# Scaling the softmax rows one attention slot later: reciprocal and product of P at the head of the next slot

## The chip, the cores and the metric

The kernel runs on one core of one Trainium2 chip. The metric is the device time of one execution in microseconds (us). The core has five engines that work from queues of their own: TensorE multiplies matrices, VectorE and ScalarE work on tiles, GpSimd does a few small things, and SyncE issues most of the transfers. Each engine takes its instructions in the order in which the program gave them out, and waits on semaphores for what others must finish first. "PE", "DVE", "ACT", "POOL" and "SP" in the rows of the profile are TensorE, VectorE, ScalarE, GpSimd and SyncE.

## The reference

One layer of an encoder over 512 tokens of width 2048, in float32:

```python
h = rmsnorm(x, g_mix)
qa, ka, va, qb, kb, vb = split(h @ w_in)
out_a = rmsnorm(mixer_a(qa, ka, va), g_out_a)   # 8 heads, 2 key/value heads, full softmax attention
out_b = rmsnorm(mixer_b(qb, kb, vb), g_out_b)   # 8 heads, three dilated windows merged
x = x + concat(out_a, out_b) @ w_out
gate, up = split(rmsnorm(x, g_ffn) @ w_gate_up)
x = x + (silu(gate) * up) @ w_down
return rmsnorm(x, g_final)
```

In each head `p = softmax(q @ k.T)` over 512 keys, and `o = p @ v`. Mixer B is done by the kernel as the same softmax with an additive mask that holds the logarithm of how often a key is seen by the three windows.

## The kernel before

**Products.** Every float32 matrix is split into a high part (a copy to a reduced format, on ScalarE) and a low part (the difference, on VectorE), and each product is three matrix products into one PSUM bank: high by high, low by high, high by low (`mm3`, lines 238 to 240). The function `split` (lines 229 and 230, or 232 and 233 with a gain) gives out the two instructions one behind the other. For streamed weights the high part is line 290 and the low part line 295; the low part of a weight tile is given out one unit after its high part.

**Units and side work.** The program is one long list of units, each of which multiplies a weight tile with the activations (12 products of 128x512 in the projection and the output projection). The main loop at the end of `encoder_block` goes through the units: it loads ahead, gives out the splits of weights to come (`prepare`), then the products of the unit, and then as much side work as a credit allows. During the projection of mixer B's q and k the credit is 1.42 a unit, from the output projection on 1.9.

**Attention slots.** The attention is side work. There are 16 heads of 4 query tiles, and one slot for each of these 64 tiles, with 9 more at the end; `head_slot(s)` gives out one slot. It does, for different heads and tiles at once: `pt` for slot s - 6 (four transposes of P on TensorE, line 580, then the high and low part of the transposed P, pTh and pTl, lines 229 and 230), `pv` for slot s - 8 (the product with v), `score` for slot s, and ahead of a new head the transposes and splits of q (`tq`) and for mixer B of k (`tk`). `score` multiplies q and k, lets VectorE find the row maxima (line 565 for mixer A, line 569 with the mask for mixer B), ScalarE the exponentials and their row sums (line 566 or 571), and VectorE the reciprocal of the sums (line 573) and P times it, in place (line 574).

Between two slots VectorE's queue gets what the program gives out there: after `tq` and `tk`, extra tasks of the slot (rotary pieces, lines 517 to 521; splits of v), then from `prepare` splits of attention outputs that were read back (class `Back`, lines 232 and 233) and of weights (line 295), and from the units the additions of finished output rows (line 960).

**Banks.** PSUM has 8 banks, kept in one queue: `bank()` takes the first, `release()` appends. A unit's accumulation holds four, the output of the current head one, and the others pass through scores and transposes. `pt` gives its bank back when pTl has been computed, `score` when the maxima (mixer A: the exponentials) have been. In the output projection four banks come free when line 960 has added the rows.

Of the kernel before, what the change touches and what calls it, by code (L numbers as in the profile page):

```python
# [67 lines left out]
def encoder_block(ctx, tc, x, g_mix, w_in, g_q_a, g_k_a, g_out_a, g_out_b, w_out, g_ffn,  # L68
# [15 lines left out]
    def slot(base, dtype=F32, shape=(P, 512)):  # L84
        return sp.tile(list(shape), dtype, tag="s", name=nm(base))
# [11 lines left out]
    def bank():  # L97
        return banks.popleft()

    def release(*tiles):  # L100
        banks.extend(tiles)
# [3 lines left out]
    def small(n=4):  # L105
        used[0] += n
        assert used[0] <= 512
        return smalls[:, used[0] - n:used[0]]
# [127 lines left out]
    def mm3(dst, a, b, start, stop, chained=False):  # L236
        (ah, al), (bh, bl) = a, b
        nc.tensor.matmul(dst, ah, bh, start=start, stop=False, skip_group_check=chained)  # L238
        nc.tensor.matmul(dst, ah, bl, start=False, stop=False, skip_group_check=chained)  # L239
        nc.tensor.matmul(dst, al, bh, start=False, stop=stop, skip_group_check=chained)  # L240

    def cols(pair, lo, n=P):
        return pair[0][:, lo:lo + n], pair[1][:, lo:lo + n]
# [285 lines left out]
    class Head:  # L529
# [27 lines left out]
        def score(self, t):  # L557
            if t == 0:
                self.negm, self.z, self.rz = small(), small(), small()
            ps = bank()  # L560
            mm3(ps, cols(self.q, t * P), self.k, True, True)
            p = slot("p")
            nmx, z, rz = self.negm[:, t:t + 1], self.z[:, t:t + 1], self.rz[:, t:t + 1]
            if self.kind == "A":
                nc.vector.tensor_reduce(nmx, ps, axis=AX.X, op=OP.max, negate=True)
                nc.scalar.activation(p, ps, AF.Exp, bias=nmx, accum_out=z)
            else:
                lo = (NT - 1 - t) * P
                nc.vector.tensor_tensor_reduce(p, ps, mask[:, lo:lo + S], -1.0, 3e38, op0=OP.add, op1=OP.min,
                                               accum_out=nmx)  # L570
                nc.scalar.activation(p, p, AF.Exp, bias=nmx, scale=-1.0, accum_out=z)
            release(ps)
            nc.vector.reciprocal(rz, z)
            nc.vector.tensor_scalar(p, p, rz, None, op0=OP.mult)
            self.p[t] = p

        def pt(self, kb):
            ps = bank()
# [42 lines left out]
    def head_at(slot):  # L621
        h, i = divmod(slot, NT)
        return (heads[h], i) if 0 <= h < len(heads) else (None, i)

    def head_slot(s):
        head, i = head_at(s - TURN_LAG)
        if head:
            head.pt(i)
        head, i = head_at(s - VALUE_LAG)
        if head:  # L630
            head.pv(i)
            if i == NT - 1:
                head.fin()
        head, i = head_at(s)
        if head:
            head.score(i)
        for lead in ("tq", "tk"):
            head, i = head_at(s + {"tq": 4, "tk": 2}[lead])
            if head and i == 0:
                getattr(head, lead)()  # L640
# [8 lines left out]
    def attention_tasks():  # L649
# [38 lines left out]
        for s in range(2 * NHA * NT + VALUE_LAG + 1):  # L688
            cost = 1.5 if s < NHA * NT else 1.2 if s < 2 * NHA * NT else 0.7
            todo += [weighed(cost, lambda s=s: head_slot(s))] + extra.get(s, [])  # L690
# [697 lines left out]
```

## Time and profile before

| | us |
|---|---|
| median of 3 runs | 2010.85 |
| range of the runs | 2010.63 to 2011.96 |
| the profiled execution's own time | 2011.22 |
| span of its instructions | 2009.4 |
| mean granted TensorE clock | 0.997 of full |

The span runs from the first instruction to the last; the rest of the execution's time, 1.8 us, lies around it. A row in order of time gives the start, the duration, the engine, the line of the kernel, the operation, the output and inputs by the program's names, and in brackets how long the engine had stood idle before it and what ended that. Where two instructions of an engine follow closely, the end of one overlaps the start of the next, so the distance from start to start says what one costs. A window row gives the busy time of each engine in a stretch of the span.

### The profile page before, as it was taken

What the parts mean: (1) busy time and instruction counts of PE and PEld (TensorE: products, weight loads), DVE (VectorE), ACT (ScalarE), POOL (GpSimd) and SP (SyncE); (2) the same over time, 40 slices, a digit from 0 to 9 for tenths busy, and PEclk for the clock granted to TensorE, in tenths of its full rate; (3) what the DMA queues carried; (4) which work ended last, traced back from release to release, by engine and by line L of the source; (5) the groups of instructions that cost most, each with busy time, mean ns of one, the idle gap of its engine ahead of it and who ended that gap; (6) DMA issues with size and microseconds to landing.
All of it is one profiled execution on the core that took longest, in us unless ns stands there. A gap on an engine that the chain in (4) does not pass through costs nothing. (4 is left out here: it accounts for less than half of the span.)

```text
span 2009.4 us, 27417 instructions
## 1 busy us (share of the span) xinstructions
PE 1984.8 (99%) x9019; PEld 1632.0 (81%) x9019; DVE 1562.4 (78%) x2781; ACT 1114.6 (55%) x1988; POOL 127.4 (6%) x157
## 2 busy tenths in 40 slices
PE   9999999999999999999999999999999999999998
PEld 7788888887788888888888888888888888788886
DVE  6877876667764698878878878878779987877967
ACT  8655345456544565555555545455555666666656
POOL 0000100000010000000000000000000121111121
PEclk9999999999999999999999999999999999999999
DMA  8577433335344645737647657558467799768765
GB/s 274 179 276 249 159 116 99 106 129 169 96 140 132 209 153 188 279 119 258 241 135 273 208 178 275 168 189 287 141 221 262 195 248 272 187 169 266 200 152 175
DMA packets 231391, 390.61 MB, mean 194 GB/s; under 512 B 21408, under 2 KB 70352, under 8 KB 231120
## 3 DMA queue, kind: packets, MB, share of 16 engines
q1 hardware_dynamic: 204880, 326.13, 48.4%
q0 software_dynamic: 14960, 33.04, 8.1%
q10 hardware_dynamic: 11408, 29.70, 4.2%
q8 instruction: 70, 1.15, 0.2%
q14 instruction: 73, 0.60, 0.1%
HBM read 325.08 MB, written 63.70 MB: 193 GB/s over the span
## 5 line engine op out<-in xcount | busy, mean ns | idle before, releaser
L238 PE MATMUL b<-tw,arena 128*128 128x512 f32 x2136 | 838.4, 392 | 2.2 <-ACT ev L1152 2.2
L239 PE MATMUL b<-tw,arena 128*128 128x512 f32 x2136 | 833.6, 390 | 2.8 <-DVE tw L777 2.6
L240 PE MATMUL b<-tw,arena 128*128 128x512 f32 x2136 | 832.9, 390 | 0.0
L774 ACT ACTIVATE tw<-raw 128x512 fp32r<-128x512 f32 x924 | 558.6, 628 | 436.6 <-DVE raw L814 285.9
L777 DVE TENSOR_TENSOR tw<-raw,tw 128x512 fp32r<-128x512 f32 x924 | 617.8, 685 | 172.4 <-ACT tw L774 169.5
L239 PEld LDWEIGHTS b<-tw,arena 128*128 128x128 f32 x2136 | 401.7, 188 | 89.2 <-DVE tw L777 7.4
L238 PEld LDWEIGHTS b<-tw,arena 128*128 128x128 f32 x2136 | 401.5, 188 | 84.6 <-ACT ev L1152 2.9
L240 PEld LDWEIGHTS b<-tw,arena 128*128 128x128 f32 x2136 | 401.4, 188 | 84.5 <-DVE arena L330 0.5
L814 DVE TENSOR_TENSOR raw<-raw,raw 128x512 f32<-128x512 f32 x528 | 360.5, 683 | 2.0 <-DMA raw<-in_w_gate_up_dram 2.0
L238 PE MATMUL b<-w,arena 128*128 128x512 f32 x368 | 146.1, 397 | 0.0
L239 PE MATMUL b<-w,arena 128*128 128x512 f32 x368 | 143.6, 390 | 0.7 <-DVE w L295 0.7
L240 PE MATMUL b<-w,arena 128*128 128x512 f32 x368 | 143.8, 391 | 0.0
L1153 POOL DMA_DIRECT2D x1d<-ev x76 | 66.4, 975 | 1150.0 <-ACT ev L1152 1135.6
L239 PEld LDWEIGHTS b<-w,arena 128*128 128x128 f32 x368 | 69.2, 188 | 15.3 <-DVE w L295 1.6
L240 PEld LDWEIGHTS b<-w,arena 128*128 128x128 f32 x368 | 69.1, 188 | 14.9
L238 PEld LDWEIGHTS b<-w,arena 128*128 128x128 f32 x368 | 69.2, 188 | 13.5
L774 ACT ACTIVATE tw<-stage 128x512 fp32r<-128x512 f32 x93 | 55.6, 627 | 41.0 <-DVE stage L814 30.6
L777 DVE TENSOR_TENSOR tw<-stage,tw 128x512 fp32r<-128x512 f32 x93 | 61.5, 684 | 13.6 <-ACT tw L774 13.6
L295 DVE TENSOR_TENSOR w<-raw,w 128x512 fp32r<-128x512 f32 x96 | 64.7, 684 | 6.0 <-ACT w L290 3.5
L230 DVE TENSOR_TENSOR pTl<-b,pTh 128x512 fp32r<-128x512 f32 x64 | 43.8, 686 | 29.6 <-ACT pTh L229 26.9
L290 ACT ACTIVATE w<-raw 128x512 fp32r<-128x512 f32 x96 | 58.3, 623 | 15.5 <-PE b L239 6.9
L357 DVE TENSOR_TENSOR pair<-pair 128x256 f32<-128x256 f32 x120 | 45.5, 420 | 26.2 <-ACT pair L1009 25.1
(189 smaller groups left out, 1748.9 us busy)
## 6 DMA issues: line engine op xcount, KB each, us to landing
raw<-in_w_gate_up_dram SPq DMA_DIRECT2D x616, 256.0 KB, 5.3
raw<-in_w_down_dram SPq DMA_DIRECT2D x176, 256.0 KB, 7.1
stage<-in_w_in_dram SPq DMA_DIRECT2D x114, 256.0 KB, 4.8
forms<-pair SPq DMA_DIRECT2D x22, 896.0 KB, 5.3
x1d<-ev POOLq DMA_DIRECT2D x76, 256.0 KB, 6.7
fr<-forms ACTq DMA_DIRECT2D x35, 512.0 KB, 6.1
raw<-in_w_in_dram SPq DMA_DIRECT2D x64, 256.0 KB, 4.4
raw<-in_w_out_dram SPq DMA_DIRECT2D x32, 512.0 KB, 4.7
```

Source lines behind the costliest of these rows:

```text
L230: nc.vector.tensor_tensor(lo, src, f32(hi), op=OP.subtract)
L238: nc.tensor.matmul(dst, ah, bh, start=start, stop=False, skip_group_check=chained)
L239: nc.tensor.matmul(dst, ah, bl, start=False, stop=False, skip_group_check=chained)
L240: nc.tensor.matmul(dst, al, bh, start=False, stop=stop, skip_group_check=chained)
L290: nc.scalar.activation(self.w[0], src, AF.Copy)
L295: nc.vector.tensor_tensor(self.w[1], self.src, f32(self.w[0]), op=OP.subtract)
L357: nc.vector.tensor_tensor(out, x, y, op=op)
L774: nc.scalar.activation(self.pair[:, 0], self.src, AF.Copy)
L777: nc.vector.tensor_tensor(self.pair[:, 1], self.src, f32(self.pair[:, 0]), op=OP.subtract)
L814: nc.vector.tensor_tensor(t[dst], t[src[0]], t[src[1]], op=OP.add if form == "m6" else OP.subtract)
L1153: nc.gpsimd.dma_start(x1_dram[2 * cb + j, row], e, accum_op=OP.add)
```

## The change

The reciprocal and the scaling leave `score` and become a function of their own, which `head_slot` calls for slot s - 1 before anything else of slot s. `score` now ends with the exponentials.

```diff
@@ -570,9 +570,12 @@
                                                accum_out=nmx)
                 nc.scalar.activation(p, p, AF.Exp, bias=nmx, scale=-1.0, accum_out=z)
             release(ps)
+            self.p[t] = p
+
+        def norm(self, t):
+            p, z, rz = self.p[t], self.z[:, t:t + 1], self.rz[:, t:t + 1]
             nc.vector.reciprocal(rz, z)
             nc.vector.tensor_scalar(p, p, rz, None, op0=OP.mult)
-            self.p[t] = p
 
         def pt(self, kb):
             ps = bank()
@@ -623,6 +626,9 @@
         return (heads[h], i) if 0 <= h < len(heads) else (None, i)
 
     def head_slot(s):
+        head, i = head_at(s - 1)
+        if head:
+            head.norm(i)
         head, i = head_at(s - TURN_LAG)
         if head:
             head.pt(i)
```

The order of the instructions on TensorE, ScalarE, GpSimd and in the transfers stays as it was; on VectorE the pair moves behind everything that is given out between two slots, to just ahead of the next slot's pTl.

## The prediction

> **What bounds the kernel now.** I read the page first, then stage windows over the attention, then the groups of VectorE, then the order of time around each stop of TensorE.
>
> From the page, the span and the TensorE total:
>
> ```profile
> span 2009.4 us, 27417 instructions
> ...
> PE 1984.8 (99%) x9019; PEld 1632.0 (81%) x9019; DVE 1562.4 (78%) x2781; ACT 1114.6 (55%) x1988; POOL 127.4 (6%) x157
> ```
>
> Windows (start:end, length, then busy us and instructions of PE, PEld, DVE, ACT, POOL, then clock, DMA share, GB/s):
>
> ```profile
> 254.00:457.00 203.00, 202.99 (x987) 167.36 (x985) 135.29 (x315) 102.54 (x219) 13.50 (x11) 1.00 0.35 114
> 457.00:479.00 22.00, 20.82 (x105) 16.48 (x103) 16.78 (x45) 14.71 (x32) 1.06 (x1) 1.00 0.59 182
> 479.00:507.00 28.00, 24.39 (x115) 19.36 (x113) 21.00 (x50) 15.22 (x31) 1.29 (x1) 0.94 0.42 139
> 507.00:540.00 33.00, 28.95 (x144) 22.71 (x145) 23.90 (x59) 16.29 (x34) 2.59 (x2) 1.00 0.37 112
> 540.00:580.00 40.00, 40.00 (x203) 32.98 (x202) 29.32 (x62) 23.80 (x48) 3.90 (x3) 1.00 0.32 102
> ```
>
> TensorE is the bound nearly everywhere. These five windows hold the attention, and in them TensorE stands still only between 457 and 540: 1.18 + 3.61 + 4.05 = 8.84 us. That is all that a better VectorE order could win, 0.44% of the time. The rest of the attention has no TensorE wait to remove, only margins to lose.
>
> The two moved instructions, grouped (busy, mean ns, idle of the engine just before them and who ended it):
>
> ```profile
> L574 DVE TENSOR_SCALAR p<-p,smalls 128x512 f32<-128x512 f32 x64 | 33.6, 525 | 2.5
> ...
> L573 DVE RECIPROCAL smalls<-smalls 128x1 f32<-128x1 f32 x64 | 10.5, 164 | 59.5 <-ACT p L566 30.1 <-ACT p L571 29.4
> ```
>
> VectorE idles 59.5 us in front of the reciprocals, 0.93 a slot, until ScalarE has finished the exponential. The question is how much of that lies under the 8.84 us. The TensorE stops, in order of time:
>
> ```profile
> 481.56 0.65 PE L580 MATMUL b<-fixed,p 128*128 128x128 f32 x4 [2.42 <-DVE pTl L230]
> 495.96 0.50 PE L238 MATMUL b<-pTh,vh 128*128 128x512 f32 x1 [0.74 <-DVE pTl L230]
> 507.08 0.50 PE L238 MATMUL b<-kTh,qTh 128*128 128x512 f32 x1 [0.52 <-DVE pTl L230]
> 511.71 0.66 PE L580 MATMUL b<-fixed,p 128*128 128x128 f32 x4 [0.45 <-DVE pTl L230]
> ...
> 521.25 0.51 PE L238 MATMUL b<-arena,arena 128*128 128x512 f32 x1 [1.10 <-DVE x L960]
> 525.46 0.65 PE L580 MATMUL b<-fixed,p 128*128 128x128 f32 x4 [0.72 <-DVE qTl L230]
> 527.26 0.51 PE L238 MATMUL b<-kTh,qTh 128*128 128x512 f32 x1 [0.45 <-DVE pTl L230]
> 539.49 0.66 PE L580 MATMUL b<-fixed,p 128*128 128x128 f32 x4 [1.25 <-DVE pTl L230]
> ```
>
> Every one ends with a VectorE instruction, mostly the low part of the transposed P, which gives a PSUM bank back. So what counts is whether that split comes earlier.
>
> **The change part by part.** No instruction is added or removed: 64 reciprocals and 64 scalings change place on VectorE's queue. No queue of DMAs is passed. The order was maximum, reciprocal, scaling, X, pTl of the next slot; it becomes maximum, X, reciprocal, scaling, pTl. X is what the program gives out between two slots: splits of q, k or v, splits of attention rows read back (L233), a weight split (L295), rotary pieces, row additions (L960). What X has to wait for decides. A slot whose X is a q and a v split, first on VectorE, then on ScalarE:
>
> ```profile
> 482.02 0.08 DVE L569 DVE_READ_ACCUMULATOR2_ANT smalls<- 128x1 f32 x1
> 482.99 0.16 DVE L573 RECIPROCAL smalls<-smalls 128x1 f32<-128x1 f32 x1 [0.88 <-ACT p L571]
> ...
> 483.59 0.68 DVE L230 TENSOR_TENSOR qTl<-b,qTh 128x512 fp32r<-128x512 f32 x1
> 484.19 0.68 DVE L230 TENSOR_TENSOR vl<-vraw,vh 128x512 fp32r<-128x512 f32 x1
> 484.79 0.68 DVE L230 TENSOR_TENSOR pTl<-b,pTh 128x512 fp32r<-128x512 f32 x1
> ```
> ```profile
> 482.14 0.72 ACT L571 ACTIVATE p<-p,smalls 128x512 f32<-128x512 f32 x1 [2.15 <-DVE smalls L569]
> ...
> 482.86 0.58 ACT L229 ACTIVATE qTh<-b 128x512 fp32r<-128x512 f32 x1
> 483.34 0.62 ACT L229 ACTIVATE vh<-vraw 128x512 fp32r<-128x512 f32 x1
> ```
>
> Reciprocal and scaling take 0.60 start to start (482.99 to 483.59). ScalarE does the high part of q behind the exponential, until 482.86 + 0.58 = 483.44. Now VectorE does its 0.60 of scaling while that runs. Afterwards it stands at the q split until about 483.48, 1.38 after the end of the accumulator read, wins 0.11 there, and then pays the 0.60 in front of pTl: pTl comes 0.49 later. With L233 first, whose high part (L232) also follows the exponential, nothing is won and pTl comes 0.60 later. If X needs nothing of ScalarE (rotary pieces, L295, whose high part is a step older), VectorE fills the 0.88 and pTl comes up to 0.88 earlier. Empty X: nothing changes.
>
> Now the stops, by the order of X in each slot. The first:
>
> ```profile
> 477.58 0.71 ACT L571 ACTIVATE p<-p,smalls 128x512 f32<-128x512 f32 x1
> ...
> 478.81 0.71 ACT L232 ACTIVATE arena<-oback,fixed 128x512 fp32r<-128x512 f32 x1
> ```
> ```profile
> 479.55 0.75 DVE L233 SCALAR_TENSOR_TENSOR arena<-oback,fixed,arena 128x512 fp32r<-128x512 f32 x1 [0.45 <-ACT arena L232]
> 480.21 0.68 DVE L295 TENSOR_TENSOR arena<-raw,arena 128x512 fp32r<-128x512 f32 x1
> 480.82 0.68 DVE L230 TENSOR_TENSOR pTl<-b,pTh 128x512 fp32r<-128x512 f32 x1
> ```
>
> 1. L233 is held by L232 (478.81 + 0.71), so 479.55 stands; L295 follows, then 0.60, then pTl. The stop of 2.42 becomes 3.02: **+0.60**.
> 2. To 495.96 VectorE runs without waiting for TensorE. The q/v slot shown gives +0.49 (1.09 by then), the next has L233 and L295, +0.60 (1.69), the third a k split, L233, L295, +0.60, but there 0.80 is swallowed by an old wait and its return:
>
> ```profile
> 495.22 0.69 DVE L230 TENSOR_TENSOR pTl<-b,pTh 128x512 fp32r<-128x512 f32 x1 [0.71 <-ACT pTh L229]
> ...
> 502.02 0.75 DVE L233 SCALAR_TENSOR_TENSOR arena<-oback,fixed,arena 128x512 fp32r<-128x512 f32 x1 [0.33 <-ACT arena L232]
> ```
>
> pTl was free to go at 495.22 - 0.71 - 0.09 of gap; 494.42 + 1.69 + 0.60 = 496.71, 1.49 later. TensorE, late by 0.60 already, loses **+0.89**.
> 3. For 507.08 the slot holds a q split, then L233 (held at 502.02 as above): **+0.60**, 2.09 in all.
> 4. The next slot's X is rotary pieces alone:
>
> ```profile
> 507.55 0.08 DVE L569 DVE_READ_ACCUMULATOR2_ANT smalls<- 128x1 f32 x1
> 508.51 0.17 DVE L573 RECIPROCAL smalls<-smalls 128x1 f32<-128x1 f32 x1 [0.88 <-ACT p L571]
> ...
> 510.96 0.69 DVE L230 TENSOR_TENSOR pTl<-b,pTh 128x512 fp32r<-128x512 f32 x1
> ```
>
> 510.96 - 508.51 - 0.60 = 1.85 of work fills the 0.88; pTl is late by 2.09 - 0.88 = 1.21 only, TensorE by 2.09, so the stop of 0.45 goes: **-0.45**, 1.64.
> 5. The row additions at a chunk's end free accumulators:
>
> ```profile
> 519.75 0.40 PE L240 MATMUL b<-arena,arena 128*128 128x512 f32 x1
> ...
> 520.45 1.41 DVE L960 SCALAR_TENSOR_TENSOR x<-b,smalls,x 128x512 f32<-128x512 f32 x2
> ```
>
> The last product ends at 520.15, L960 starts 0.30 later. It can start 0.27 sooner, no more, as it needs that product: **-0.27** of the 1.10, 1.37 in all. The scaling then stands behind the pair, so pTl and the next maximum are late by 1.37 + 0.60 = 1.97.
> 6. The q split after it:
>
> ```profile
> 522.98 0.08 DVE L569 DVE_READ_ACCUMULATOR2_ANT smalls<- 128x1 f32 x1
> ...
> 524.71 0.69 DVE L230 TENSOR_TENSOR qTl<-b,qTh 128x512 fp32r<-128x512 f32 x1
> ```
>
> 523.06 + 1.97 + 1.38 = 526.41 against 524.71, 1.70 later: **+0.33** beyond 1.37.
> 7. Two splits, then 0.60, then pTl: 1.70 + 0.60 = 2.30 late, so 527.26 moves by **+0.60**. The stop before 539.49 follows its own ScalarE chain and moves along unchanged.
>
> Sum +2.3 us on the profiled execution (span 2009.4, time 2011.22): 2013.5. The median of the runs lies 0.37 below that execution, so I forecast 2013.1. A measurement of this kernel tells about 0.2%, 4.0 us, from no change; this is inside.
>
> Costed at nothing: 254 to 457, where VectorE is busy 135.29 of 203 us and TensorE stops 0.01; and 540 to 580. Without that cover each of some five slots with splits or L960 there costs 0.49 to 0.60, at most 2.4 us; a gain is excluded, since TensorE is busy 40.00 of 40.00.
>
> **The rivals.** *The wait goes and none follows.* Were the high parts ready when VectorE reaches X, the stops it ends at 481, 496, 507, 511, 525 and 527 (5.30) and 0.27 at L960 go: 2005.3. It decides from about three quarters of that. Against it: both ScalarE rows of the q/v slot start behind the exponential. Chance 0.10.
>
> *Nothing moves.* VectorE's delays and gains cancel ahead of TensorE: 2010.9. For it: the slots with L295 or rotary pieces alone win what the others lose. Chance 0.16.
>
> *Slower beyond 4 us.* Between 540 and 580 the late pTl meets a TensorE without spare banks: 2.3 + 2.4 = 4.7, 2015.5; it decides from 1.7 of the 2.4. For it: VectorE waits there for little but the exponential. Against: no stop now. Chance 0.16.
>
> *The clock.* After the 2.42 us stop TensorE ran slowly:
>
> ```profile
> 482.00:486.00 4.00, 4.00 (x13) 3.14 (x12) 3.08 (x9) 2.30 (x5) 0.00 (x0) 0.57 0.01 5
> ```
>
> 0.43 x 4.00 = 1.72 us of work lost, now hidden as VectorE sets the pace there. A second such stretch, after a stop that grows to 1.6 near 496 or follows 527, would be uncovered: 2.3 + 1.7 = 4.0, 2014.9, on the bound. Chance 0.08. [...]
>
> **How the numbers follow.** Forecast 0.50. Same: 0.50 + 0.16 + half of the clock's 0.08 = 0.70; slower 0.16 + 0.04 = 0.20; faster 0.10. The range takes in no change, the two slow cases and a little beyond each, and leaves the full gain out: 2009.0 to 2016.0.
>
> **What would show it.** The idle in front of the reciprocals falls from 59.5 us to under 15; instead VectorE waits in front of qTl, kTl, vl and L233 for ScalarE, over 20 us together (24 q and k splits at up to 1.38). The stop near 481 grows to about 3.0, that near 511 goes, the one at L960 shrinks to about 0.8. TensorE's idle from 457 to 540 is about 11. I am wrong if that idle falls below 6, if stops appear before 457 or after 540, or if the q and k splits come without a wait.

## The result and the profile after

| | before | after |
|---|---|---|
| median of 6 runs of each, us | 2012.2 | 2017.33 |
| lowest and highest, us | 2010.63, 2016.39 | 2016.9, 2021.22 |
| the profiled execution: time, span, us | 2011.22, 2009.4 | 2017.18, 2015.4 |
| mean granted TensorE clock | 0.997 | 0.996 |

The ratio is 1.0028, 95% interval 1.0019 to 1.0038: slower by 5 us, where 2.3 were forecast, and above the range's end of 2016.0. Three runs of the kernel before were added here, and its median with them is 2012.2 in place of the 2010.85 above.

The top of the page of the kernel after:

```profile
span 2015.4 us, 27422 instructions
...
PE 1987.7 (99%) x9019; PEld 1634.3 (81%) x9019; DVE 1562.6 (78%) x2781; ACT 1114.2 (55%) x1988; POOL 127.9 (6%) x157
```

The windows of the kernel after, with the columns of the prediction's:

```profile
254.00:457.00 203.00, 203.00 (x989) 167.68 (x988) 136.23 (x314) 101.78 (x216) 13.70 (x11) 1.00 0.35 114
457.00:479.00 22.00, 20.63 (x103) 16.46 (x101) 16.44 (x46) 13.99 (x29) 1.06 (x1) 1.00 0.48 148
479.00:507.00 28.00, 22.55 (x98) 18.13 (x98) 17.43 (x40) 16.53 (x34) 1.29 (x1) 0.88 0.48 166
507.00:540.00 33.00, 30.58 (x144) 23.98 (x144) 25.62 (x64) 14.59 (x31) 1.29 (x1) 0.95 0.33 102
540.00:580.00 40.00, 38.91 (x197) 31.69 (x196) 27.92 (x61) 22.43 (x48) 3.87 (x3) 1.00 0.26 84
```

TensorE stands still for 1.37 + 5.45 + 2.42 = 9.24 us from 457 to 540 (8.84 before), and now for 1.09 from 540 to 580, where it was busy for 40.00 of 40.00. Stops of 9.24 + 1.09 - 8.84 = 1.49 do not make 5 us; the clock of 0.88 and 0.95 (0.94 and 1.00 before) and places outside these windows have a part in it.

VectorE's group of reciprocals, and then its waits from 245 to 585 us (in total, times, the longest), of the kernel after:

```profile
L577 DVE RECIPROCAL smalls<-smalls 128x1 f32<-128x1 f32 x64 | 10.2, 159 | 12.4 <-ACT p L566 6.8 <-ACT p L571 5.7
```
```profile
DVE pTl L230 <- ACT pTh L229: 36.1, 28, 3.0
DVE qTl L230 <- ACT qTh L229: 17.8, 13, 1.4
DVE kTl L230 <- ACT kTh L229: 9.9, 7, 1.5
...
DVE arena L233 <- ACT arena L232: 6.6, 7, 2.7
```

The idle in front of the reciprocals fell from 59.5 to 12.4 us, and VectorE now waits 17.8 + 9.9 + 6.6 = 34.3 us for the high parts of the splits that come first (1.9 before, all of it in front of L233).

**Where the 5 us are.** Each execution is cut at three instructions of TensorE that every kernel has: the first transposes of q (L542), the first transposes of finished output rows (`b<-fixed,x`), and a stop in the down projection that ends with ScalarE's `ev`. The stretch between the first two is the attention and holds every instruction that was moved. In an execution of the kernel before:

```profile
242.83 0.60 PE L542 MATMUL b<-fixed,qA 128*128 128x128 f32 x4
...
644.27 0.60 PE L1006 MATMUL b<-fixed,x 128*128 128x128 f32 x4
```

All parts in us, from rows like these; the labels are those of the experiments, `before` and `after` the executions above:

| kernel | start | attention | behind it | tail | span |
|---|---|---|---|---|---|
| before | 242.56 | 401.37 | 1084.34 | 281.13 | 2009.4 |
| before_second | 242.83 | 401.44 | 1084.68 | 279.75 | 2008.7 |
| before_third | 242.60 | 401.47 | 1084.69 | 278.64 | 2007.4 |
| after | 244.05 | 405.61 | 1085.45 | 280.29 | 2015.4 |
| after_second | 242.66 | 405.18 | 1085.90 | 279.56 | 2013.3 |
| after_third | 242.96 | 405.96 | 1086.27 | 279.81 | 2015.0 |
| e_odd | 242.73 | 401.04 | 1082.51 | 279.82 | 2006.1 |
| odd_third | 243.21 | 401.24 | 1082.21 | 279.64 | 2006.3 |
| e_even | 242.91 | 405.55 | 1084.70 | 280.24 | 2013.4 |
| e_mixerA | 244.43 | 400.31 | 1084.58 | 281.38 | 2010.7 |
| e_last_heads | 243.62 | 403.35 | 1084.69 | 279.54 | 2011.2 |
| last_second | 242.85 | 402.01 | 1085.28 | 279.46 | 2009.6 |
| e_not_last | 242.65 | 403.39 | 1086.08 | 281.58 | 2013.7 |
| not_last_third | 242.88 | 403.48 | 1085.24 | 280.20 | 2011.8 |
| e_behind_score | 243.40 | 397.93 | 1084.21 | 279.46 | 2005.0 |
| e_splits_first | 242.90 | 402.30 | 1085.22 | 279.48 | 2009.9 |
| one_third_head | 242.90 | 402.41 | 1082.12 | 278.77 | 2006.2 |
| one_fifth_head | 244.66 | 401.34 | 1086.15 | 279.95 | 2012.1 |

By the means of the three executions of each, the change costs 405.58 - 401.43 = 4.15 us in the attention and 1085.87 - 1084.57 = 1.30 behind it. Start and tail vary by up to 2.5 us between executions of one kernel; the 1.49 by which the start of the profiled execution after lies later than before's is of that kind, as two other executions of it start at 242.66 and 242.96.

### The profile page after: what moved, and what is told of

Same layout as the page of the kernel before. It is cut to its first block, busy times and chain, and to the rows that moved or that the text cites. A ratio compares the mean times of both kernels' runs of the same rounds, so it can differ in the third digit from the quotient of the medians.

```text
span 2015.4 us, 27422 instructions
## 1 busy us (share of the span) xinstructions
PE 1987.7 (99%) x9019; PEld 1634.3 (81%) x9019; DVE 1562.6 (78%) x2781; ACT 1114.2 (55%) x1988; POOL 127.9 (6%) x157
## 4 chain that ended last, share of the span: by engine, by line
PE 88%; DVE 5%; DMA 3%; ACT 2%; issue 1%; ACTq 0%; POOL 0%; SPq 0%; POOLq 0%; DVEq 0%
PE b L238 28%; PE b L239 28%; PE b L240 28%; DMA raw<-in_w_down_dram 2%; DVE tw L783 2%; PE b L583 1%; DVE raw L820 1%; PE b L1087 1%; DVE arena L1138 0%; ACT tw L780 0%; PE b L319 0%; PE b L1012 0%; DVE pTl L230 0%; DMA x<-x1d 0%; PE b L542 0%
## 5 line engine op out<-in xcount | busy, mean ns | idle before, releaser
L239 PEld LDWEIGHTS b<-tw,arena 128*128 128x128 f32 x2136 | 401.4, 188 | 90.3 <-DVE tw L783 9.1
L238 PEld LDWEIGHTS b<-tw,arena 128*128 128x128 f32 x2136 | 401.4, 188 | 85.3 <-ACT ev L1158 2.9
```

## The experiments

**The new order in the odd tiles alone, and in the even tiles alone.** In the even tiles what the program gives out between two slots begins with a q split (tile 0) or, in mixer B, a k split (tile 2); in the odd tiles with none.

```diff
+            if t % 2 != 1:      # e_even: != 0
+                self.norm(t)
...
         head, i = head_at(s - 1)
-        if head:
+        if head and i % 2 == 1: # e_even: == 0
             head.norm(i)
```

> The deferral for query tiles 1 and 3 of each head only; tiles 0 and 2 scale at once, as before. The splits of q and k are given out in slots of tiles 0 and 2, so here no deferred pair stands behind one. Theory of the waits (the loss comes from the pair queued behind splits that ScalarE has not begun): near the kernel before, -1 to +1.5 us, VectorE's waits in front of qTl and kTl almost gone, the stop near 481 us still about 3.0 as its slot holds a read-back split (L233). Rival of the clock (the loss is the number of half-rate stretches of 1.7 us each, whatever the order): +2 to +5 us, if three stretches stay. Rival that the deferral as such costs: half of the whole change, about +2.5 us.

> The deferral for query tiles 0 and 2 only, the slots with the splits of q and k. Theory of the waits: most of the loss of the whole change, +2 to +5 us, over 20 us of VectorE waits in front of qTl and kTl, and none of the gain in the slots of weight splits alone. Rival that the deferral as such costs: half, about +2.5 us, with no difference to the odd tiles. Rival of the clock: follows the number of half-rate stretches, 1.7 us for each beyond the one of the kernel before.

Measured: the odd tiles alone 2008.18 us, ratio 0.9983 [0.9974, 0.9992]; the even tiles alone 2016.09, ratio 1.0024 [1.0015, 1.0033]. The attention of the even tiles is 4.1 us longer, as in the changed kernel; that of the odd ones 0.2 to 0.4 shorter. So the loss in the attention comes with the slots that begin with a q or a k split. Most of it follows the mechanism of the prediction: VectorE's waits for qTh and kTh (17.8 and 8.4 us with the even tiles) are not there with the odd ones. But 0.86 of the 4.1 arise at one stop, before 542.82, that another cause lengthens (see the part on why the prediction was wrong). The 3 us that the odd tiles win are not in the attention at all: 2.1 to 2.4 of them lie behind it, where nothing was moved. That is taken up below.

**Mixer A alone.**

```diff
+            if self.kind != "A":
+                self.norm(t)
...
-        if head:
+        if head and head.kind == "A":
             head.norm(i)
```

> The deferral in mixer A's heads alone (slots up to about 412 us); mixer B scales at once. Cover as the prediction had it: TensorE has no stop before 457 us although VectorE waits some 10 us in front of qTl there; the time is that of the kernel before, within 1 us. Rival, that the deferral costs in every slot: half of the loss, +2.5 us.

Measured: 2012.27 us, ratio 1.0001 [0.9992, 1.0010]; no stop of TensorE before 457. That part of "costed at nothing" holds. The attention is even 1.1 us shorter than before's, but hardly through the new order: in this execution the clock granted to TensorE is 1.00 from 479 to 507, where before's is 0.94, with one stretch at half rate (0.57 from 482 to 486). What such a stretch is worth is read from `last_second` below.

**The last two heads of mixer B alone, and all but these.** Their slots are the ones behind 534 us.

```diff
+            if self.kind == "A" or self.h < 6:      # e_not_last: kind "B" and h >= 6
+                self.norm(t)
...
-        if head:
+        if head and head.kind == "B" and head.h >= 6:      # e_not_last: not that
             head.norm(i)
```

> The deferral in the last two heads of mixer B alone, about 540 to 570 us. As the prediction costed it: nothing, no stop of TensorE after 540 us. Rival (the cover there is thin, as the changed kernel's two stops at 556 and 558 us say): two stops of 0.8 us together between 550 and 560 us, +0.8 us.

> The deferral everywhere but in the last two heads of mixer B, the complement of the run of those alone. Theory that the stretch after 540 us carries about half of the loss (two stops there, behind a margin of 0.15 us that the kernel before had between the pTl of 550.45 us and the product of 551.29): +1.5 to +3 us over the kernel before, no stop of TensorE after 545 us. Theory that the loss is the sum of the steps up to 527 us: the whole +5. If the half-rate stretches decide: +1.7 for each that later stops don't hide.

The stops of TensorE from 530 to 560 us, first with the last two heads alone, then with all but these:

```profile
540.96 0.66 PE L585 MATMUL b<-fixed,p 128*128 128x128 f32 x4 [1.67 <-DVE pTl L230]
553.72 0.50 PE L238 MATMUL b<-pTh,vh 128*128 128x512 f32 x1 [0.70 <-DVE pTl L230]
555.15 0.50 PE L238 MATMUL b<-kTh,qTh 128*128 128x512 f32 x1 [0.45 <-ACT sq L611]
```
```profile
541.58 0.66 PE L585 MATMUL b<-fixed,p 128*128 128x128 f32 x4 [1.18 <-DVE pTl L230]
```

The stops behind 540 belong to the last two heads, and to nothing else. The attention is 1.98 longer with them alone (403.35 against 401.37) and 1.96 without them (403.39 and 403.48 against 401.47 and less): the two sum to the 4 of the changed kernel. The times say more than that: 2015.92, ratio 1.0017 [1.0008, 1.0026], and 2015.55, ratio 1.0022 [1.0012, 1.0032], 4.9 us each by the medians and 3.4 and 4.4 by the ratios. The rest had to lie outside the attention.

**Both kernels once more on one chip.** No edit.

> The kernel before once more, for a second execution's clock. [...] If the half rate costs its 1.7 us each time, the attention is 1.7 shorter without it.

> The changed kernel once more. The stops near 478, 484 and 499 and those of 556 and 558 us come again within 0.3 us, as VectorE's order makes them; the number of half-rate stretches may differ from three. If the stretches only take the place of later stops, the attention (first transposes of q to first transposes of the output rows, 405.6 us in the first execution) is within 1 us of that; if they add up, 1.7 us shorter for each one less.

> The deferral in the last two heads once more, as the runs' median lies 2.9 us above the execution that was profiled (2013.02). [...]

This pair shows the change cleanest: the starts are 0.17 us apart, and from 455 to 560 both have TensorE at half rate in one stretch only (products of 0.63 us in place of 0.39, starting from 483.13 to 484.83 before and from 483.61 to 485.74 after). The execution of the changed kernel, its two marks of the attention and the stops between them, less two that the kernel before has too (0.64 near 459 and 0.45 near 478):

```profile
242.66 0.60 PE L542 MATMUL b<-fixed,qA 128*128 128x128 f32 x4
...
476.66 0.50 PE L238 MATMUL b<-pTh,vh 128*128 128x512 f32 x1 [0.54 <-DVE pTl L230]
...
482.53 0.85 PE L583 MATMUL b<-fixed,p 128*128 128x128 f32 x4 [3.05 <-DVE pTl L230]
497.80 0.50 PE L238 MATMUL b<-pTh,vh 128*128 128x512 f32 x1 [1.65 <-DVE pTl L230]
509.29 0.50 PE L238 MATMUL b<-kTh,qTh 128*128 128x512 f32 x1 [0.93 <-DVE pTl L230]
522.26 0.50 PE L238 MATMUL b<-arena,arena 128*128 128x512 f32 x1 [0.58 <-DVE x L966]
524.11 0.66 PE L583 MATMUL b<-fixed,p 128*128 128x128 f32 x4 [0.18 <-DVE pTl L230]
526.77 0.66 PE L583 MATMUL b<-fixed,p 128*128 128x128 f32 x4 [0.62 <-DVE qTl L230]
529.16 0.50 PE L238 MATMUL b<-kTh,qTh 128*128 128x512 f32 x1 [1.04 <-DVE pTl L230]
542.26 0.65 PE L583 MATMUL b<-fixed,p 128*128 128x128 f32 x4 [2.10 <-DVE pTl L230]
554.64 0.50 PE L238 MATMUL b<-pTh,vh 128*128 128x512 f32 x1 [0.34 <-DVE pTl L230]
556.06 0.50 PE L238 MATMUL b<-kTh,qTh 128*128 128x512 f32 x1 [0.45 <-ACT sq L609]
...
647.84 0.60 PE L1012 MATMUL b<-fixed,x 128*128 128x128 f32 x4
```

Set against the starts of the same instructions in the kernel before, the shift between the two grows by these steps (the numbers are the prediction's):

| place | start before | start after | shift grows by | predicted |
|---|---|---|---|---|
| a product near 384 | 384.00 | 383.53 | -0.30 | 0 |
| a new stop near 477 | 476.60 | 476.66 | +0.53 | 0 |
| 1 | 481.84 | 482.53 | +0.63 | +0.60 |
| 2 | 496.26 | 497.80 | +0.85 | +0.89 |
| 3 | 507.39 | 509.29 | +0.36 | +0.60 |
| 4 | 512.02 | 513.30 | -0.62 | -0.45 |
| 5 | 521.56 | 522.26 | -0.58 | -0.27 |
| 6 | 525.76 | 526.77 | +0.31 | +0.33 |
| 7 | 527.56 | 529.16 | +0.59 | +0.60 |
| "moves along unchanged" | 539.83 | 542.26 | +0.83 | 0 |
| "costed at nothing" | 552.47 | 556.06 | +1.16 | 0 |
| first output rows | 644.27 | 647.84 | -0.02 | 0 |
| sum | | | +3.74 | +2.3 |

With the last two heads alone, in the execution `last_second`, TensorE's clock is 1.00 in every window from 478 to 490. Two windows of it, below the same two of the kernel before in `before_second` (the clock is the third number from the end):

```profile
482.00:484.00 2.00, 2.00 (x8) 1.71 (x8) 1.08 (x5) 1.57 (x4) 0.00 (x0) 0.50 0.04 13
484.00:486.00 2.00, 2.00 (x7) 1.59 (x6) 2.00 (x4) 0.73 (x2) 0.00 (x0) 0.66 0.00 0
```
```profile
482.00:484.00 2.00, 2.00 (x12) 1.70 (x11) 1.08 (x5) 1.72 (x4) 0.00 (x0) 1.00 0.03 12
484.00:486.00 2.00, 2.00 (x10) 1.64 (x10) 2.00 (x4) 0.59 (x2) 0.00 (x0) 1.00 0.00 0
```

Up to there the order of the two is the same. At 485.26 TensorE is 1.68 us ahead; at the stop near 496, which grew from 0.74 to 1.52, 0.96 of that is left, and 1.21 near 507. So VectorE's chain hides 0.5 to 0.7 of the 1.7 us that the stretch of `before_second` loses (0.50 x 2.00 + 0.34 x 2.00 = 1.68), and 1.0 to 1.2 go through.

**The order with the q and k splits ahead of the score, and the reciprocal behind it.**

```diff
-        head, i = head_at(s)        # e_splits_first: tq and tk stand ahead of score
-        if head:
-            head.score(i)
         for lead in ("tq", "tk"):
             ...
+        head, i = head_at(s)
+        if head:
+            head.score(i)
```
```diff
     def head_slot(s):               # e_behind_score: norm stands behind score, ahead of tq and tk
-        head, i = head_at(s - 1)
-        if head:
-            head.norm(i)
...
             head.score(i)
+        head, i = head_at(s - 1)
+        if head:
+            head.norm(i)
```

> The changed kernel, with one thing taken from what makes VectorE wait: the transposes and splits of q and k of the next head are given out ahead of the slot's score, so that ScalarE's high parts stand ahead of the exponential in its queue. Theory of the waits: VectorE's idle in front of qTl and kTl falls from 27.7 us to under 8, and the loss goes: 3 to 6 us below the changed kernel, at or a little below the kernel before; the stop near 481 us stays about 3, as L233 is not moved. Rival of the clock: as the number of half-rate stretches, whatever these waits do. Rival that the deferral as such costs: as slow as the changed kernel.

> Reciprocal and scaling of the slot before are given out right behind the score of this slot, so the pair runs while the exponential of this slot does and stands in front of the splits again. Theory of the waits: pTl is never later than in the kernel before, and up to 0.88 us earlier in slots without a split; VectorE's idle in front of the reciprocals under 2 us; TensorE's idle in the attention falls from 8.8 to 4 to 6 us, the time by 2 to 6 us below the kernel before. Rival that the deferral as such costs: as slow as the changed kernel, +5 us. Rival of the clock: gains only as the stop near 481 falls so far that its half-rate stretch goes, another 1 us.

Measured: splits ahead of the score 2012.76 us, ratio 1.0006 [0.9997, 1.0016], attention 402.30; no stop is left behind 540, and the waits of L233 double to 12.9 us. Those in front of qTl and kTl fell to 7.3 + 2.3 = 9.6 us, not under 8, and the mean granted clock of this execution is 0.996, against before's 0.997, so the two orders are not compared cleanly by it. Reciprocal and scaling behind the next slot's maxima 2008.24, ratio 0.9984 [0.9975, 0.9992], attention 397.93, which is 3.5 us shorter than before's. It beats both kernels. There the pair fills the time in which ScalarE computes the high parts, and the low parts follow without having been put behind. The stops of TensorE near 511 and 521 are gone, and those near 525 and 539 shrank to 0.49 and 0.42.

**The clock by itself.** Two programs that leave out the whole block and write a copy of an input tile to every output row: dense products on TensorE, broken by stops of VectorE of six lengths and then by pairs of stops (first), or by short stops and runs of transposes (second).

```diff
+        for k in STOPS:                          # e_stops: 0 to 5 additional VectorE additions
+            stop(ps, k)
+            n += 1
+            ps = dense(DENSE + 5 * (n % 4))
...
+        for k, t in ((0, 0), (0, 4), (0, 8), (0, 12), (0, 20), (None, 12), (None, 24), (1, 4)):   # e_turns
+            if k is not None:
+                stop(ps, k)
+                dense(1)
+            turns(t)
+            n += 1
+            ps = dense(DENSE + 5 * (n % 4))
```

> The disputed cost by itself: nothing of the block is computed and the output holds a copy of a tile of x. Runs of 46 to 61 dense 128x512 products are parted by stops in which VectorE does 2 to 7 instructions of 0.6 us (about 1.5 to 4.5 us), six times each; then pairs of stops with 4 or 9 products between them. [...]

> The clock by itself, second part: nothing of the block is computed and the output holds a copy of a tile of x. Dense runs are parted by a stop of 1.1 us followed by 0, 4, 8, 12 or 20 transposes of 128x128, by 12 or 24 transposes without a stop, and by a stop of 1.8 us with 4 transposes, eight times each. [...]

Three stops of the first program, and two windows behind the last of them:

```profile
18.09 11.86 PE L93 MATMUL b<-b,a 128*128 128x512 f32 x51 [1.18 <-DVE a L100]
31.79 13.01 PE L93 MATMUL b<-b,a 128*128 128x512 f32 x56 [1.84 <-DVE a L100]
47.36 13.00 PE L93 MATMUL b<-b,a 128*128 128x512 f32 x49 [2.56 <-DVE a L100]
```
```profile
49.00:50.00 1.00, 1.00 (x4) 0.81 (x3) 0.00 (x0) 0.00 (x0) 0.00 (x0) 0.50 0.00 0
53.00:54.00 1.00, 1.00 (x6) 0.84 (x5) 0.00 (x0) 0.00 (x0) 0.00 (x0) 1.00 0.00 0
```

Behind the stops of 1.18 and 1.84 us the products took 0.23 us each (11.86 for 51, 13.01 for 56). Behind that of 2.56 the 49 took 13.00, 1.6 us longer than at this pace, and the clock in the windows of 1 us from 48 on is 0.90, 0.50, 0.50, 0.50, 0.89 and 1.00: by these, some 0.20 + 3.00 + 0.22 = 3.4 us at half rate. In the second program, 12 and 24 transposes alone (1.47 and 2.79 us of them) were each followed by products of 0.23 us:

```profile
90.97 1.47 PE L106 MATMUL t<-ident,raw 128*128 128x128 f32 x12
92.20 12.98 PE L95 MATMUL b<-b,a 128*128 128x512 f32 x56
105.01 2.79 PE L106 MATMUL t<-ident,raw 128*128 128x128 f32 x24
107.55 14.08 PE L95 MATMUL b<-b,a 128*128 128x512 f32 x61
```

The mean granted clock is 0.906 over the 1093.4 us of the first program and 0.995 over the 959.7 us of the second, so an estimate from the means, with the clock at 1.00 or 0.50 throughout, is that (1 - 0.906) x 2 x 1093.4 = 206 us of the first lie at half rate, and (1 - 0.995) x 2 x 959.7 = 10 us of the second.

In the kernel's own executions the length of a stop does not tell by itself whether half rate follows. With a stop of 2.42 us the clock is 0.57 from 482 to 486 in `before`, and 1.00 from 479 to 507 in `e_mixerA`; with one of 3.06 it is 0.50 from 484 to 486 in `after`, and with one of 3.05 it is 1.00 from 478 to 496 in `not_last_third`. The second program was to explain the stretch of the changed kernel with a stop of 1.04 us (0.50 from 532 to 534 in `after`) and did not; that stays open.

**Does the rest stick to the kernel?** No edit; the same four kernels on one chip.

> The kernel before, looked at once more on the chip of three others, to part the time in three: up to the first transposes of q (about 242.8 us), from there to the first transposes of the output rows (the attention), and from there to the end. Attention theory (all that the change costs lies between 457 and 560 us): the attention is 401.4 us again and the rest 1364 to 1366 us. Rival (something behind the attention, in which no instruction was moved, sticks to a kernel): the rest is 1364.4 again within 0.3, and the changed kernels of this row stay longer.

> The changed kernel once more. Attention theory: the attention is 405.2 us with one stretch at half rate, up to 405.6 with three; stops near 478 [0.54], 498 [1.65], 542 [2.1] and 555 and 556 [0.34 and 0.45] again; the rest lies as the kernel before's of the same row does, 1364 to 1366. Rival: the rest is longer than the other's by 1 us or more.

> The new order everywhere but in the last two heads of mixer B, a second look at this kernel. Attention theory: the attention is 403.4 again, none of its stops after 542; the time is 2012.5 to 2013.5, as the 1367.7 us behind the attention of the earlier look was of that execution. Rival: the rest is 1367 or more again, so 2015 to 2016, and what the change costs lies in good part behind the attention.

> The new order in tiles 1 and 3 alone, a second look. Attention theory: the attention is 401.0 again (0.4 under the kernel before), and the rest comes back to 1364 to 1366: 2009.5 to 2011. Rival: the rest is 1362.3 again, so 2007 to 2008, and the gain of this kernel is not in the attention.

The attention repeated (401.47, 405.96, 403.48, 401.24), and so did the stretch behind it in three of the four, against the attention theory: 1084.69 before, 1086.27 after, 1082.21 with the odd tiles. Without the last heads it is 1085.24 after 1086.08, and the time 2013.56 after 2015.55. What differs there are short stops at the weight splits of the down projection near 1700, three in the kernel before (0.56 + 0.22 + 0.58 = 1.36 us), five in the changed one (0.71 + 0.22 + 0.58 + 0.23 + 0.58 = 2.32), none with the odd tiles. Set against `before_third` instruction by instruction, all of the difference arises at these stops: 2.4 us less from 1699 to 1720 with the odd tiles, 1.6 more from 1688 to 1698 in the changed kernel. The first of each in `before_third` and `after_third`:

```profile
1699.16 0.50 PE L239 MATMUL b<-tw,arena 128*128 128x512 f32 x1 [0.56 <-DVE tw L777]
```
```profile
1694.40 0.50 PE L238 MATMUL b<-tw,arena 128*128 128x512 f32 x1 [0.71 <-ACT tw L780]
```

**One reciprocal and one scaling.** The built programs show what could carry this. SyncE's instructions stand in the same order in the changed kernel, in the one with the odd tiles and in the two below as in the kernel before, but the framework packs the tiles of the weight stream into SBUF by the order in which the program takes and frees them, and a load waits for the last reader of what lay in its place. In the changed kernel 159 of the 176 loads of the down projection have another place than before. Two kernels move one single pair each, in slots where TensorE does not stop:

```diff
+            if 4 * (8 * (self.kind == "B") + self.h) + t not in (8,):   # one_fifth_head: (16,)
+                self.norm(t)
...
+        if s - 1 in (8,):                                             # one_fifth_head: (16,)
+            head.norm(i)
```

> One reciprocal and one scaling moved, those of tile 0 of the third head of mixer A (slot 8, in the stretch 254 to 457 where TensorE does not stop); all the rest in the order of the kernel before. In the built program this alone deals the buffers of the weight stream anew: in the down projection the load that must wait for VectorE's weight split of about 1700 us is the 1394th raw tile and no more the 1388th, as in the kernel with the new order in tiles 1 and 3. Dealing theory: the attention stays at 401.4 us, the stretch from its end to the stop of 1.68 near 1727 falls from 1084.5 to 1082.3, with no stop at the weights' splits near 1700, and the time falls by about 2: 2008 to 2009. Rival (the time behind the attention hangs on the execution, or on the attention's length): 1084.5 again and no difference in time.

> The same with tile 0 of the fifth head of mixer A (slot 16) in place of the third's. This deals the buffers nearly as the changed kernel has them: the 1369th raw tile of the weights already waits for a split of VectorE, the 1388th for that of about 1700 us. Dealing theory: the attention stays at 401.4 us, the stretch behind it becomes 1085.4 to 1086.3 as in the changed kernel, its stops at the weights' splits near 1700 come to 1.6 to 2.3 us, and the time rises by about 1: 2011.5 to 2012.5. Rival: 1084.5 and no difference in time.

What the first of these does to SyncE's loads in the built program; DVE behind "waits" is a wait for VectorE to have read a buffer:

```
-L267 DMA raw_1386_13814<-in_w_down_dram 128x512 [waits DMAHW3_49]
+L267 DMA raw_1386_13814<-in_w_down_dram 128x512 [waits DMAHW3_49,DVE_49]
-L267 DMA raw_1388_13939<-in_w_down_dram 128x512 [waits DMAHW1_49,DVE_49]
+L267 DMA raw_1388_13939<-in_w_down_dram 128x512 [waits DMAHW1_49]
-L267 DMA raw_1394_14093<-in_w_down_dram 128x512 [waits DMAHW7_49]
+L267 DMA raw_1394_14093<-in_w_down_dram 128x512 [waits DMAHW7_49,DVE_49]
```

SyncE's waits for VectorE's weight splits from 1600 to 1690 us (total, times, longest), in the kernel before (`before_third`), in `one_third_head` and in `one_fifth_head`:

```profile
SPq L267 <- DVE tw L777: 23.3, 5, 19.9
```
```profile
SPq L267 <- DVE tw L785: 20.4, 14, 9.3
```
```profile
SPq L267 <- DVE tw L785: 25.4, 11, 19.6
```

The same 20 us of the down projection, 980 us behind the first output rows, in the same three (the last number is GB/s):

```profile
1624.07:1644.07 20.00, 20.00 (x90) 16.57 (x89) 14.46 (x23) 12.38 (x21) 5.18 (x6) 1.00 1.00 267
```
```profile
1625.31:1645.31 20.00, 20.00 (x90) 16.57 (x89) 14.47 (x23) 12.38 (x21) 5.16 (x6) 1.00 1.07 312
```
```profile
1626.00:1646.00 20.00, 20.00 (x90) 16.58 (x89) 14.47 (x23) 12.37 (x21) 5.18 (x6) 1.00 1.02 273
```

Measured: the pair of slot 8 alone 2008.0 us, ratio 0.9985 [0.9976, 0.9994], stretch behind the attention 1082.12, no stop near 1700. The pair of slot 16 alone 2013.92, ratio 1.0012 [1.0003, 1.0020], stretch 1086.15, five stops. One moved pair, worth nothing where it stands, makes the kernel 3.2 us faster or 2.7 slower; 2.45 and 1.58 of that lie behind the attention, where no engine's order differs and all that it changed is where tiles lie in SBUF and which waits follow from that. The other 1.1 of the second kernel has no place in its profile but the start (244.66), which lies ahead of the moved pair. In the first, six more loads pass before SyncE's long wait (19.9 us falls to 9.3), and the transfers run at 312 in place of 267 GB/s while TensorE still has work. The dealing theory gave 1082.3 and 1085.4 to 1086.3. It missed two numbers: the time of `one_fifth_head` (2013.92, where 2011.5 to 2012.5 were expected) and the attention of `one_third_head`, which is 402.41, not 401.4. There TensorE was at half rate for longer:

```profile
486.00:488.00 2.00, 2.00 (x7) 1.53 (x7) 1.01 (x4) 1.61 (x4) 0.00 (x0) 0.59 0.47 157
```
```profile
486.00:488.00 2.00, 2.00 (x11) 1.61 (x10) 0.79 (x4) 1.82 (x4) 0.00 (x0) 1.00 0.71 205
```

(`one_third_head` above, `before_third` below.) From 480 to 488, in steps of 2 us, the clock is 0.70, 0.50, 0.50 and 0.59 in the first and 1.00, 0.56, 0.59 and 1.00 in the second, with a stop of 2.42 us in both; what makes the difference is not shown.

## Why the prediction was wrong

**What bounds the kernel now** was read rightly, and so was the mechanism: q, k and L233 splits that wait for ScalarE now stand ahead of the scaling. The signs it named came: idle in front of the reciprocals 12.4 (under 15), waits for high parts 34.3 (over 20), the stop near 481 3.05 to 3.06 (3.0), that near 511 gone, L960's (now L966) 0.57 to 0.58 (0.8). So did the sign it named for being wrong: stops after 540. One sign was missed: TensorE's idle from 457 to 540 is 9.24 in the profiled execution and 83.00 - 73.31 = 9.69 in `after_second`, not about 11. The stop of 2.10 in `after_second` ends at 542.26 and so lies behind that border, and steps 1 to 7 sum to less than forecast.

The prediction's list of stops begins at 481. Two come before it in the same window, 0.73 at 459.68 and 0.45 at 477.74, and the second ends with ScalarE's square of the head output (L603), so "every one ends with a VectorE instruction" is not quite so. Neither enters its sum.

**Steps 1 to 7.** Predicted +2.3, measured 0.63 + 0.85 + 0.36 - 0.62 - 0.58 + 0.31 + 0.59 = +1.54 in the clean pair. Steps 1, 2, 6 and 7 came within 0.04; 3 cost 0.24 less, and the gains of 4 and 5 were larger by 0.17 and 0.31. In front of them a stop of 0.54 near 477 was missed (pv's opening product, waiting for the bank of a late pTl), and a gain of 0.30 near 384.

**"Costed at nothing" is the step that failed first.** For 254 to 457 it held. For 540 to 580 it cost 1.16 us in place of nothing, and it was TensorE's 40.00 of 40.00 that misled: a busy TensorE says that there was no wait, not how much room there was. The rows of the kernel before had the room, VectorE's pTl and pv's opening product, which takes the bank that pTl frees:

```profile
550.45 0.69 DVE L230 TENSOR_TENSOR pTl<-b,pTh 128x512 fp32r<-128x512 f32 x1 [0.27 <-ACT pTh L229]
```
```profile
551.29 0.48 PE L238 MATMUL b<-pTh,vh 128*128 128x512 f32 x1
```

pTl ends at 551.14, and the product starts 0.15 later. In that slot the k split comes first, and the changed kernel has this (`after_second`):

```profile
552.11 0.69 DVE L230 TENSOR_TENSOR kTl<-b,kTh 128x512 fp32r<-128x512 f32 x1 [1.42 <-ACT kTh L229]
...
553.31 0.15 DVE L577 RECIPROCAL smalls<-smalls 128x1 f32<-128x1 f32 x1
553.50 0.49 DVE L578 TENSOR_SCALAR p<-p,smalls 128x512 f32<-128x512 f32 x1
553.91 0.68 DVE L230 TENSOR_TENSOR pTl<-b,pTh 128x512 fp32r<-128x512 f32 x1
```

1.42 of waiting for kTh, and 0.60 from the reciprocal's start to pTl's. A pTl that is 0.5 late cannot fit into 0.15. Half of the cost of +1.16 arises here: 0.56 at this product. The other 0.61 arises at the next score product (556.06). It waits for a bank that ScalarE gives back when it has squared the head's output (`sq`), and the square starts late:

```profile
555.41 0.60 ACT L609 ACTIVATE sq<-b 128x512 f32<-128x512 f32 x1 [0.91 <-PE b L239]
```

In the built program of the changed kernel this `sq` lies in SBUF where the pTl lay that the second part of the late product reads (554.98), and waits for that. So it is in the programs of `e_even` and `e_last_heads`, which have the stop too; in those of `before`, `e_odd` and `e_not_last`, which don't have it, `sq` lies elsewhere. So the 0.61 comes with the dealing of buffers as well as with the late product, and no run parts the two.

The rival "slower beyond 4 us" happened, at half of its bound of 2.4, and the new stop near 477 has the same form.

**"The stop before 539.49 ... moves along unchanged"** failed by +0.83, but not through VectorE. The stop follows a pTh that waits for a transfer out of the buffer it writes into:

```profile
535.74 0.42 SPq L504 DMA_DIRECT2D vraw<-vB  x1
535.83 0.34 ACTq L603 DMA_DIRECT2D oB<-oT  x1
...
540.88 0.60 ACT L229 ACTIVATE pTh<-b 128x512 fp32r<-128x512 f32 x1 [2.49 <-DMA oB<-oT]
```

From issue to pTh it is 540.88 - 535.83 = 5.05 us here, 538.46 - 534.23 = 4.23 in `before_second`, 540.21 - 536.07 = 4.14 in `e_not_last`; the first profile after had a stop of 0.28 in place of 2.10. The stop of 2.1 came in `e_even` and two of three executions after, and in none of three before (1.25 to 1.30). The traces show one thing that goes with it. In all executions of the changed kernel, of `e_even` and of the last two heads alone, SyncE issues a load of v (`vraw<-vB`, the first row above) ahead of this transfer. In all others but `e_splits_first` (2.06 us behind it) the load comes 12 us or more behind, as in `before_second`:

```profile
546.92 0.37 SPq L504 DMA_DIRECT2D vraw<-vB  x1
```

Where pTh waits for the transfer, it is 4.55 to 5.07 us from issue to pTh in the five executions with the load 0.02 to 0.09 us ahead, and 4.14 to 4.38 in the ten with it behind; in the first profile after the load was 0.87 ahead and it is 3.24. In the built programs of `after`, `e_even` and `e_last_heads` this load goes to another place in SBUF and waits for an earlier product than in those of `before`, `e_odd` and `e_not_last`, so the buffers have a part here too. No run moves the load alone, so that it slows the transfer is not shown.

**"No queue of DMAs is passed"** is true of the order and missed the waits. The loads of the weights are dealt other buffers, 1100 us later that goes with 1.30 on the mean, and it was in no term, rival or bound. `one_fifth_head` shows the effect alone: 1.58 us there.

**The clock.** The prediction took the stretch at half rate near 482 as hidden; about 1.0 to 1.2 of its 1.7 are not (`last_second`). The kernel before has it in all three executions (a clock of 0.57 from 482 to 486 in `before`, of 0.50 and 0.66 in the two halves of that in `before_second`, of 0.56 and 0.59 in `before_third`), so this cancels where the changed kernel has one such stretch too. The profiled execution after had three, with stops of 3.06, 1.95 and 1.04 us (a clock of 0.50 from 484 to 486, 501 to 503 and 532 to 534), so the rival's further ones do come; but `after_second` had one as before and still lost 3.74, so the loss doesn't need them. What they cost in the profiled one can't be read off, as the transfer named above took another time there too.

**The sum.** 1.54 in steps 1 to 7, 0.23 ahead of them, 0.83 and 1.16 behind, less 0.02, make 3.74; it is 4.15 on the mean of three, and 1.30 in the down projection: 5.4, against 5.1 between the medians. Of the 5.4, 0.61 + 0.83 + 1.30 = 2.7 go with other places of buffers, which the prediction did not consider; only for the last 1.30 does a run move the buffers without the rest. Open is why the kernels with and without the last two heads have medians some 2 to 3 us above what their attention and the stretch behind it give. Their executions spread over 6.6 and 4.4 us, and the one profiled at 2015.55 has a tail of 281.58 against 280.20 in `not_last_third`, at a mean clock of 0.997 against 0.998. A further stretch at half rate is an estimate there, from `before`: its tail is 281.13 against 279.75 in `before_second`, and its clock 0.62, 0.50, 0.50 and 0.68 in the four windows of 1 us from 1728 to 1732.

## What to carry to other kernels

An engine that is 100% busy in a stretch is no cover for a delay on the engine that feeds it (here TensorE was busy for 40.00 of 40.00 us, and a late pTl cost 0.56): look up, per slot, how long after the feeder's last instruction the product really starts, and let a delay cost all that exceeds that margin. When work is put off on an in-order engine, put it where the engine would otherwise wait, here between the next maxima and the splits (`e_behind_score`, 3.2 us faster), and not in front of the instruction that frees a bank. And before a difference of 0.2% is put down to an edit, cut both traces at common instructions: a moved pair of small instructions can change how a packer deals buffers a thousand us later, which went with -2.45 and +1.58 us there, of -3.2 and +2.7 between the medians, for one pair that costs nothing where it stands.

## What was not expected of the hardware

With some stops TensorE's granted clock was 0.50 for some 3.4 us, and with others of the same length it was not. By windows of 1 us it is at half rate for 3.4 us from 482.4 and from 1728.2 in `before`, with stops of 2.42 and 1.68 us, and for 3.4 us each from 483.5, 500.5 and 531.3 in `after`, with stops of 3.06, 1.95 and 1.04. It stayed at 1.00 with a stop of 2.42 us in `e_mixerA` (479 to 507), with one of 3.05 in `not_last_third` (478 to 496) and with one of 1.66 in `after` (1733 to 1741). Behind 2.79 us of transposes in the second bare program the products kept their 0.23 us each. What decides is not shown. So a kernel with such stops can have executions that differ by more than 1 us with the same instructions, as those of `e_last_heads` and `last_second` do: the attention takes 403.35 and 402.01, and in the second the clock is 1.00 from 478 to 490. That the first had one stretch at half rate is an estimate, from the 1.0 to 1.2 us that one costs there.
